# Spreading reciprocal roots over partitions: a store to DRAM and a broadcast read in place of eight products

## The chip, the cores and the metric

The kernel runs on one core of a Trainium2 chip. The metric is the device time of one execution in microseconds. PE is the engine of matrix products, DVE, ACT and POOL are the engines that work element by element, SP issues most of the DMAs. Each engine works through its own instructions in order, and waits where an instruction needs what another engine or a DMA has not finished. Profile lines name kernel lines as L381, and tiles by the program's names.

## What is computed

One layer of an encoder: RMS norm, one projection to q, k, v and a gate, two-dimensional neighbourhood attention, an output projection with the residual, and a last RMS norm. x has 2048 rows of 1024 numbers, all in float32.

```python
def rmsnorm(x, g):
    y = xf * lax.rsqrt(jnp.mean(xf * xf, axis=-1, keepdims=True) + RMS_EPS)
    return y * g

h = rmsnorm(x, norm_0)
q, k, v, gate = split(h @ w_in_0, 4)            # 1024 x 4096
o = neighbourhood_attention(q, k, v, rpb_0)     # 32 x 64 grid, windows of 8 x 16, 16 heads of 64
x = x + (o * silu(gate)) @ w_out_0
return rmsnorm(x, norm_f)
```

## The kernel before

**Products.** Each float32 factor is split into a rounded high part and a rest (ACT rounds, DVE subtracts, L445 and L446), and a product is made of three: high by high, high by rest, rest by high. Blocks of 128 by 512 are combined in the manner of Strassen, with seven products of blocks in place of eight (`seven_products`). One such product is twelve instructions on PE (L361). A unit is one pair of heads of q, k or gate: seven products in the order 1, 6, 2, 7, 5, 4, 3, in three PSUM banks that several of them share. Between them the results are read out: `keep` by ACT (L369), `add` by DVE (L374), `out_` by DVE (L379) with a product on POOL behind it (L381), `evac` by DVE (L296). A gate tile then goes through ACT (L307) and DVE (L308) and is stored by SP (L309); q and k are stored by SP (L314).

**Stages.** Stage one works on columns 0 and 1, the first 1024 rows of x transposed: first the values (`products_v`, L706), then twelve units, k of four pairs, and then q and gate in turn. Stage two works on the other 1024 rows: values first (`values_of`, L487, in four pairs of row tiles), then twelve units. Attention, the output projection and the last norm follow.

**Where the norm enters.** In stage one the products are made of x itself, times the gains, and the rows' reciprocal roots are multiplied in when the results leave PSUM: the tile rb[c] (c is 0 or 1) holds the 512 roots of column block c, the same on all 128 partitions. DVE reads it in `evac`, POOL in `out_`. Stage two multiplies rb[2] and rb[3] into the blocks of x before they are split (`normed`, L441).

**How rb is made.** The sums of squares are taken with rows on partitions (`square`), so the roots come out in rt with rows on partitions (`stats`: a few small instructions on DVE and POOL). To spread them, `diagonal(c)` multiplies the identity by four columns of rt on POOL and splits the result on ACT and DVE; `spread_rstd(c)` multiplies a tile of ones with both parts on PE and copies the result out of PSUM with ACT. For c of 0 and 1 it is written in the order in which k is stored (`lay("k", ...)`), and `reorder_rstd` rewrites it for q and gate when the four k units are done. The order matters because q, k and gate are stored in another order of rows than the one in which the products make them: `of` reads with a step of eight words, and `lay` writes runs:

```python
def of(kind, t):
    return t.rearrange("p (r c s) -> p r s c", c=8, s=8) if kind == "k" else t.rearrange("p (n s) -> p s n", s=8)
```

**What sets the order.** The schedule is written by hand. In the values of stage one a small planner places jobs between products: `job(ready, due, ops, f)` gives the earliest step, the due step and a cost of 2.8 steps for each op; a step is one instruction on PE. From there on, `also(n, i)` is called behind product i of unit n (n is 0 for the last unit of the stage), and `begun` holds functions for the first calls. In stage two, functions are handed to `pair` and called behind every twelve products of the values. Stores are put off by a number of products (`store(key, lag, f)`, carried out by `due`), and go to SP's queue at that point, so SP's order is the order of these calls. `ahead(i)` loads weights and forms factors of later products. Tiles are taken from pools that turn round: rb has three places, the first two of which are used by rows for the sums of squares and the third by a sum of the values.

Of the kernel before, what the change touches and what calls it, by code (L numbers as in the profile page):

```python
# [10 lines left out]
F32 = mybir.dt.float32  # L11
F32R = mybir.dt.float32r
BF16 = mybir.dt.bfloat16
I32 = mybir.dt.int32
AF = mybir.ActivationFunctionType
OP = mybir.AluOpType
# [44 lines left out]
def build(ctx, tc, x, xr, xt, wg, tab, w_out, n0, nf, out):  # L61
    nc = tc.nc
    ctx.enter_context(tc.manual_schedule())
    dram = ctx.enter_context(tc.tile_pool(name="dram", bufs=1, space=DRAM))
# [2 lines left out]
    sgd = [dram.tile([128, S], F32, name=f"sgd{p}") for p in range(NP)]  # L67
    vd = [dram.tile([4, S, 128], F32, name=f"vd{u}") for u in range(2)]
    ogd = [dram.tile([128, 4, NP, 128], F32, name=f"ogd{T}") for T in range(4)]
    wod = {f: dram.tile([128, 4, 2, 512], F32, name=f"wod{f}") for f in ("T1", "T2", "T3", "T4")}  # L70

    def pool(name, bufs):
# [3 lines left out]
    one = ctx.enter_context(tc.tile_pool(name="one", bufs=1))  # L76
# [27 lines left out]
    ev = pool("ev", 8)  # L104
    rbp = pool("rbp", 3)
# [3 lines left out]
    def bank(n, name):  # L109
        return banks.tile([128, n], F32, name=name, tag="bank")  # L110
# [5 lines left out]
        nc.tensor.matmul(zp, z[:, :128], z, start=True, stop=True)  # L116
    ident = one.tile([128, 128], F32, name="ident")
    make_identity(nc, ident)
    ones = one.tile([128, 128], F32, name="ones")
    nc.vector.memset(ones, 1.0)  # L120
    onesr = one.tile([128, 128], F32R, name="onesr")
    rt = one.tile([128, 16], F32, name="rt")
    rth = one.tile([128, 8], F32, name="rth")
    g0 = one.tile([128, NK], F32, name="g0")
# [15 lines left out]
    rb = {}  # L140
# [46 lines left out]
        if cs[0] < 2:  # L187
            nc.gpsimd.tensor_scalar(rth[:, 4 * cs[0]:4 * cs[0] + n], y, 0.5, 1.0, op0=OP.mult, op1=OP.mult)

    dgs = {}  # L190

    def diagonal(c):
        dg = ev([128, 512], F32, "dg")
        for i in range(4):
            nc.gpsimd.tensor_scalar(dg[:, i * 128:(i + 1) * 128], ident, rt[:, 4 * c + i:4 * c + i + 1], 1.0,
                                    op0=OP.mult, op1=OP.mult)
        dgs[c] = h, l = ev([128, 512], F32R, "dgh"), ev([128, 512], F32R, "dgl")
        nc.scalar.activation(h, dg, AF.Copy)
        nc.vector.tensor_tensor(l, dg, h.bitcast(F32), OP.subtract)

    def spread_rstd(c):
        p = bank(512, "prb")
        h, l = dgs.pop(c)
        nc.tensor.matmul(p, onesr, h, start=True, stop=False)
        nc.tensor.matmul(p, onesr, l, start=False, stop=True)
        rb[c] = rbp([128, 512], F32, "rb")
        if c < 2:
            nc.scalar.activation(lay("k", rb[c]), of("k", p), AF.Copy)
        else:
            nc.scalar.activation(rb[c], p, AF.Copy)  # L210

    def reorder_rstd(c):
        t = rbp([128, 512], F32, "rb")
        nc.scalar.activation(t.rearrange("p (s r c) -> p s r c", r=8, c=8),
                             rb[c].rearrange("p (r s c) -> p s r c", s=8, c=8), AF.Copy)
        rb[c] = t


    units_two = [(k, j) for j in range(4) for k in "kqg"]
    attending = [False]  # L220
# [42 lines left out]
    def of(kind, t):  # L263
        return t.rearrange("p (r c s) -> p r s c", c=8, s=8) if kind == "k" else t.rearrange("p (n s) -> p s n", s=8)

    def lay(kind, t):
        return t.rearrange("p (r s c) -> p r s c", s=8, c=8) if kind == "k" else t.rearrange("p (s n) -> p s n", s=8)
# [25 lines left out]

    def evac(kind, hp, c, p, then):
        tmp = ev([128, 512], F32, "tmp")
        nc.vector.tensor_tensor(lay(kind, tmp), of(kind, p), lay(kind, rb[c]), OP.mult)  # L296
        then.append(lambda: give(kind, hp, c, tmp))

    def give(kind, hp, c, t, bank_=False):
# [29 lines left out]
    def seven_products(us, c0, X1, also, lead=lambda i: 6, homes={}):  # L329
# [46 lines left out]
        def out_(n, a, c, P, u, then):  # L376
            kind, j = us[n]
            tmp = ev([128, 512], F32, "tmp")
            nc.vector.tensor_tensor(lay(kind, tmp), of(kind, B[n, P]), lay(kind, u), OP.add)  # L379
            if c0 == 0:  # L380
                nc.gpsimd.tensor_tensor(tmp, tmp, rb[c], OP.mult)  # L381
            then.append(lambda: give(kind, 2 * j + a, c, tmp))

        def ahead(i, more=0):
# [140 lines left out]
    def stage_one():  # L525
# [39 lines left out]
        begun = []  # L565

        def also(n, i):
            m = n + len(us) - 1
            if begun:
                begun.pop(0)()  # L570
            if (m, i) == (4, 0):
                reorder_rstd(0)
                reorder_rstd(1)
            if m < 8 and i == 2:
                more_rows[m] = xp([128, 512], F32, "row"), xp([128, 512], F32, "row")
                for j in range(2):
                    nc.sync.dma_start(more_rows[m][j], xr[(8 + m) * 128:(9 + m) * 128, 512 * j:512 * j + 512])
            if m < 8 and i == 6:
                for j, t in enumerate(more_rows.pop(m)):
                    square(8 + m, j, t)  # L580
                if m in (3, 7):
                    stats(2 + m // 4)
            if (n, i) == (-3, 1):
                diagonal(2)
            if (n, i) == (-3, 6):
                spread_rstd(2)
            if (n, i) == (-3, 5):
                spot2 = mkp([128, 3, 512], F32, "spot")
                L2["x11"] = [spot2[:, k] for k in range(3)] + [lp([128, 512], F32, "land")]
                for k in range(4):  # L590
                    load_x(2, "x11", k, L2["x11"][k])
            if (n, i) == (-2, 2):
                L2["x21"] = [xp([128, 512], F32, "land") for _ in range(4)]
                for k in range(4):
                    load_x(2, "x21", k, L2["x21"][k])
            if (n, i) in norms:
                f, k = norms[n, i]
                normed(f, 2, k, L2[f][k])
            if (n, i) == (-3, 4):
                diagonal(3)  # L600
            if n == 0:
                if i == 0:
                    for a, b in ((0, 0), (1, 0), (0, 1)):
                        load_v0(0, a, b)
                    X2["B11"] = [(xs([128, 512], F32R, "h"), xs([128, 512], F32R, "l")) for _ in range(4)]
                    for k in (0, 1):
                        split_to(*X2["B11"][k], L2["x11"][k], None)
                elif i == 1:
                    for a, b in ((1, 1), (0, 2), (1, 2)):
                        load_v0(0, a, b)  # L610
                    for k in (2, 3):
                        split_to(*X2["B11"][k], L2["x11"][k], None)
                    split_v(0, 0, 0)
                    split_v(0, 1, 0)
                elif i == 2:
                    X2["B21"] = [(xs([128, 512], F32R, "h"), xs([128, 512], F32R, "l")) for _ in range(4)]
                    split_v(0, 0, 1)
                elif i == 3:
                    split_v(0, 1, 1)
                    L2["x12"] = [vh([128, 512], F32, "land") for _ in range(4)]  # L620
                    for k in range(4):
                        load_x(2, "x12", k, L2["x12"][k])
                    for a in range(2):
                        load_v0(0, a, 3)
                elif i in (4, 5):
                    for k in (0, 1) if i == 4 else (2, 3):
                        split_to(*X2["B21"][k], L2["x21"][k], None)
                    if i == 5:
                        split_v(0, 0, 2)
                        split_v(0, 1, 2)  # L630
# [6 lines left out]
        parts_ = slice(0, 256), slice(256, 512)  # L637
        load_v0(0, 0, 0, cols=parts_[0], by=nc.scalar)
        load_x(0, "x11", 0, land["x11"][0], parts_[0])
        nc.scalar.activation(onesr, ones, AF.Copy)  # L640
        load_v0(0, 1, 0, cols=parts_[0])
        load_x(0, "x11", 0, land["x11"][0], parts_[1])
        load_v0(0, 0, 0, cols=parts_[1])
# [85 lines left out]
        def add_v(to, P, t, x, made=None):  # L729
            U[to, t] = made or U[x, t]  # L730
            nc.vector.tensor_tensor(U[to, t], B[bank_of[P], t], U[x, t], OP.add)
# [38 lines left out]
        def job(ready, due_, ops, f, *a):  # L770
            jobs.append((ready, due_, len(jobs), ops, f, a))
# [11 lines left out]
        for P, f, x, src, ready in ((5, "T1", t1, "x12", 46), (6, "T2", less, "x22", 84), (7, "T3", less, "x11", 130),  # L783
                                    (4, "T4", less, "x21", 130)):
            start = {5: 96, 6: 144, 7: 192, 4: 240}[P] - 12
# [29 lines left out]
            at(113 + 9 * i, square_rows, h)  # L815
        job(255, 255, .3, stats, 0, 1)
        at(250, ahead, -9)
        job(314, 303, 0.7, diagonal, 0)
        job(323, 312, 0.7, diagonal, 1)
        job(280, 284, 0, ahead, -8)  # L820
        job(282, 304, 1, ahead, -7)
        job(286, 308, 1, ahead, -6)
# [27 lines left out]
        for k in range(2):  # L850
            if k == 0:
                WV_["A11", 0] = wp([128, 2, 512], F32R, "wh"), wp([128, 2, 512], F32R, "wl")
                for h in range(2):
                    for a in ((1, 0) if h == 0 else ()):
                        t = raw_v("A11", a, 0).rearrange("p (k c) -> p k c", c=256)
                        s = slice(a * 256, a * 256 + 256)
# [11 lines left out]
            for a in range(2):  # L868
                t = raw_v("A11", a, 0).rearrange("p (k c) -> p k c", c=256)
                s = slice(a * 256, a * 256 + 256)  # L870
# [10 lines left out]
        while plan:  # L881
            plan.pop(0)[1]()
        VR.clear()
        begun.extend([lambda: [spread_rstd(0)] + [add_v(2, 3, t, 2) for t in (0, 1)],
                      lambda: [spread_rstd(1)] + [add_v(2, 3, t, 2) for t in (2, 3)]]
                     + [lambda ts=ts: [scaled(0, 4 + t, U, (2, t)) for t in ts] for ts in ((0, 1), (2, 3))])
        run()

# [875 lines left out]
```

## Time and profile before

| | |
|---|---|
| median of three runs | 1004.39 us (1003.68 to 1004.54) |
| the profiled execution | 1003.49 us, of which the span of the profile is 1001.7 us |
| busy: PE, DVE, ACT, POOL | 991.6, 727.5, 523.1, 197.7 us |
| granted clock of PE | 0.999 |
| stage one, values | to 83 us |
| stage one, units | 83 to 314 us |
| stage two, values and units | 314 to 588 us |

All figures below come from one profiled execution. The busy time of PE is a sum of pipelined instructions, and their rows are longer than the distance between two starts. In the rows of groups stand the line, the engine, the operation, the output and inputs, shape and count, then the busy time and the mean of one in ns, and then the idle time ahead of them with what ended it. In timelines the columns are the start and the length in us, the line and the operation; in brackets stands the idle time of the engine ahead of it, and what ended that. SPq stands for the DMAs that SP issues.

### The profile page before, as it was taken

To read this page: it belongs to the slowest core of one execution; us is meant where nothing else is said; L and a number is where in the kernel's file an instruction comes from. 1 tells how busy PE (TensorE), PEld (TensorE's weight loads), DVE (VectorE), ACT (ScalarE), POOL (GpSimd) and SP (SyncE) were. 2 spreads that over 40 slices of the span, in tenths; PEclk is the share of its full clock that TensorE was granted. 3 is DMA by queue.
4 is the path that set the end of the run, shared out by engine and by line. 5 is a ranking of instruction groups with operands and counts; after the bars stand their busy time and mean duration, and the time that the engine had idled before them with its cause. 6 is when DMAs were issued, how large, how long until landed. Compare 5 with 4: busy or idle time off the path is not lost.

```text
span 1001.7 us, 21635 instructions
## 1 busy us (share of the span) xinstructions
PE 991.6 (99%) x8080; PEld 802.0 (80%) x8080; DVE 727.5 (73%) x1557; ACT 523.1 (52%) x1316; POOL 197.7 (20%) x340
## 2 busy tenths in 40 slices
PE   9999999999999999999999999999999999999997
PEld 6888888888888888888888877777777777788885
DVE  6997666767798895776676565576767777666786
ACT  6767233333334452432433256777878777673253
POOL 0012323324321300000000012323333333320010
PEclk9999999999999999999999999999999999999999
DMA  9439445352736245655745588899988999989922
GB/s 315 135 96 271 139 138 146 118 157 92 202 91 205 76 142 151 220 183 170 236 162 160 167 250 285 298 329 348 299 269 282 316 309 294 318 282 354 355 94 84
DMA packets 124928, 213.82 MB, mean 213 GB/s; under 512 B 11352, under 2 KB 45528, under 8 KB 124824
## 3 DMA queue, kind: packets, MB, share of 16 engines
q1 hardware_dynamic: 123752, 209.96, 65.1%
q0 software_dynamic: 640, 2.10, 0.5%
q8 instruction: 63, 1.03, 0.4%
q14 instruction: 41, 0.34, 0.1%
q10 hardware_dynamic: 432, 0.40, 0.1%
HBM read 153.69 MB, written 58.72 MB: 212 GB/s over the span
## 4 chain that ended last, share of the span: by engine, by line
PE 90%; DVE 6%; issue 1%; ACT 1%; POOL 1%; DMA 0%; SPq 0%; DVEq 0%; ACTq 0%
PE pp L361 43%; PE o L1184 8%; PE pt L1463 7%; PE pv L706 7%; PE s L1120 6%; PE ph L1165 5%; PE pv L1019 5%; PE po L1379 3%; PE po L1383 3%; PE po L1381 3%; DVE l L446 1%; DVE land L441 1%; ACT h L445 1%; DVE land L963 1%; DMA raw<-in_wg_dram 0%
## 5 line engine op out<-in xcount | busy, mean ns | idle before, releaser
L361 PE MATMUL pp<-h,f 128*128 128x512 f32 x768 | 247.0, 389 | 0.8 <-DVE u L374 0.8
L361 PEld LDWEIGHTS pp<-h,f 128*128 128x128 f32 x768 | 144.2, 188 | 31.2 <-DVE u L374 1.2
L361 PE MATMUL pp<-four,f 128*128 128x512 f32 x648 | 156.8, 389 | 0.3 <-DVE u L374 0.3
L361 PE MATMUL pp<-l,f 128*128 128x512 f32 x384 | 149.5, 389 | 0.0
L361 PEld LDWEIGHTS pp<-four,f 128*128 128x128 f32 x648 | 121.5, 188 | 26.0 <-DVE u L374 0.9
L1148 POOL TENSOR_SCALAR x<-x,st 128x264 f32<-128x264 f32 (+1 forms) x192 | 96.7, 521 | 224.4 <-DVE st L1139 223.7
L1134 ACT ACTIVATE x<-x,st 128x264 f32<-128x264 f32 (+1 forms) x256 | 124.4, 487 | 21.2 <-DVE st L1129 21.2
L381 POOL TENSOR_TENSOR tmp<-tmp,rb 128x512 f32<-128x512 f32 x36 | 59.4, 1651 | 162.6 <-DVE tmp L379 128.2
L1129 DVE CUSTOM_DVE_ANT_0 x<-s,em 128x264 f32<-128x264 f32 (+1 forms) x256 | 89.4, 404 | 1.8 <-PE s L1120 1.8
L1168 DVE COPY pta<-ph 120x512 f32<-120x512 f32 (+5 forms) x96 | 56.0, 638 | 44.5 <-PE ph L1165 44.2
L1184 PEld LDWEIGHTS o<-pta,vt 120*64 120x64 f32 (+2 forms) x1024 | 68.5, 137 | 19.7 <-DVE st L1129 12.2
L361 PEld LDWEIGHTS pp<-l,f 128*128 128x128 f32 x384 | 72.1, 188 | 14.9
L1184 PE MATMUL o<-pta,vt 120*64 120x192 f32 (+5 forms) x1024 | 83.4, 316 | 0.0
L369 ACT ACTIVATE p<-pp 128x512 f32<-128x512 f32 x24 | 14.3, 597 | 120.4 <-PE pp L361 114.1
L1168 ACT ACTIVATE pta<-ph 120x512 f32<-120x512 f32 (+5 forms) x96 | 49.1, 558 | 43.9 <-PE ph L1165 43.9
L446 DVE TENSOR_TENSOR f<-raw,f 128x512 fp32r<-128x512 f32 x77 | 55.2, 719 | 23.2 <-ACT f L445 23.2
L1120 PE MATMUL s<-kt,qt 64*32 64x264 f32 (+1 forms) x2048 | 64.3, 374 | 0.0
L445 ACT ACTIVATE f<-raw 128x512 fp32r<-128x512 f32 x77 | 47.6, 624 | 30.3 <-PE pp L361 16.6
L379 DVE TENSOR_TENSOR tmp<-pp,u 128x512 f32<-128x512 f32 x48 | 33.1, 690 | 39.0 <-PE pp L361 34.4
L1165 PEld LDWEIGHTS ph<-ident,x 64*120 64x120 f32 (+2 forms) x1536 | 46.2, 128 | 11.3 <-issue 10.2
L361 PE MATMUL pp<-sixths,f 128*128 128x512 f32 x216 | 52.9, 389 | 0.0
L1165 PE MATMUL ph<-ident,x 64*120 64x64 f32 (+2 forms) x1536 | 50.7, 219 | 0.0
(246 smaller groups left out, 1855.6 us busy)
## 6 DMA issues: line engine op xcount, KB each, us to landing
raw<-in_wg_dram SPq DMA_DIRECT2D x120, 256.0 KB, 4.6
em<-in_tab_dram SPq DMA_DIRECT2D x16, 912.0 KB, 7.8
em<-in_tab_dram SPq DMA_DIRECT2D x16, 528.0 KB, 7.3
row<-in_xr_dram SPq DMA_DIRECT2D x32, 256.0 KB, 3.4
sgd<-sg SPq DMA_DIRECT2D x32, 256.0 KB, 2.8
qt<-qd SPq DMA_DIRECT2D x32, 256.0 KB, 5.5
sgt<-sgd SPq DMA_DIRECT2D x32, 256.0 KB, 8.8
ogd<-og SPq DMA_DIRECT2D x32, 256.0 KB, 4.0
```

The source lines that it names most:

```text
L361: nc.tensor.matmul(B[n, P], t[:, int(m == 2), c], x[k][int(m == 1)], start=P in (1, 6, 5) and k == 0 and m == 0, stop=k == 3 and m == 2, s ...
L381: nc.gpsimd.tensor_tensor(tmp, tmp, rb[c], OP.mult)
L446: nc.vector.tensor_tensor(l, t, h.bitcast(F32), OP.subtract)
L706: nc.tensor.matmul(B[bank_of[P], t], a[:, t * 128:t * 128 + 128], b, start=P == bank_of[P] and k == 0 and m == 0, stop=k == 3 and m == 2, ...
L1120: nc.tensor.matmul(pst[s][h * 32:h * 32 + 32], qt[e, q:q + 32], keys.rearrange("p r (s c) -> p s r c", c=8), start=True, stop=True)
L1129: nc.vector.tensor_tensor_reduce(X[i, C][s], ps, em, -1.0, 1e38, OP.add, OP.min, st[:, o:o + 1])
L1134: nc.scalar.activation(X[i, C][s], X[i, C][s], AF.Exp, bias=st[:, o:o + 1], scale=-1.0, accum_out=st[:, 4 + o:5 + o])
L1148: nc.gpsimd.tensor_scalar(X[i, C][s], X[i, C][s], st[:, o:o + 1], 1.0, op0=OP.mult, op1=OP.mult)
L1165: nc.tensor.transpose(to_, XF[2 * m + C // 2, C][s][q, j * k:j * k + k], ident[q, q])
L1168: (nc.vector.tensor_copy if h else lambda o, i_: nc.scalar.activation(o, i_, AF.Copy))(to[:k, :, 2 - j, h, c], at[h][:k, :, c])
L1184: nc.tensor.matmul(o[s * 64:s * 64 + 64, g0 * 64:g1 * 64 + 64].rearrange("d (g q) -> d g q", q=64), vt[:k, strip, s * 64:s * 64 + 64], t[: ...
L1463: nc.tensor.matmul(B[n, P], t[:, int(m == 2), c], WO[uses[P][1], k][int(m == 1)], start=P in (1, 6, 5) and k == 0 and m == 0, stop=k == 3 ...
```

## The change

The roots are stored to DRAM in the order of rows and read back by all 128 partitions at once. `diagonal`, the eight products with ones, the copies out of PSUM, `reorder_rstd` and the tiles ones and onesr are gone. `store_rstd` is issued on POOL, the read on SP. rb now always lies in the order of rows, so `evac` and `out_` read it with `of`, by a step of eight words. The reads of rb[0] and rb[1] move from behind the first product of the units into the planned part; those of rb[2] and rb[3] stay at their places in the order of calls.

```diff
+    rd = [dram.tile([512], F32, name=f"rd{c}") for c in range(4)]
...
-    ones = one.tile([128, 128], F32, name="ones")
-    nc.vector.memset(ones, 1.0)
-    onesr = one.tile([128, 128], F32R, name="onesr")
...
-    def diagonal(c):
...
+    def store_rstd(*cs):
+        for c in cs:
+            nc.gpsimd.dma_start(rd[c].rearrange("(t p) -> p t", p=128), rt[:, 4 * c:4 * c + 4])
 
     def spread_rstd(c):
-        p = bank(512, "prb")
-        h, l = dgs.pop(c)
-        nc.tensor.matmul(p, onesr, h, start=True, stop=False)
-        nc.tensor.matmul(p, onesr, l, start=False, stop=True)
         rb[c] = rbp([128, 512], F32, "rb")
-        if c < 2:
-            nc.scalar.activation(lay("k", rb[c]), of("k", p), AF.Copy)
-        else:
-            nc.scalar.activation(rb[c], p, AF.Copy)
-
-    def reorder_rstd(c):
...
+        nc.sync.dma_start(rb[c], bass.AP(tensor=rd[c].tensor, offset=rd[c].offset, ap=[[0, 128], [1, 512]]))
...
     def evac(kind, hp, c, p, then):
-        nc.vector.tensor_tensor(lay(kind, tmp), of(kind, p), lay(kind, rb[c]), OP.mult)
+        nc.vector.tensor_tensor(lay(kind, tmp), of(kind, p), of(kind, rb[c]), OP.mult)
...
             if c0 == 0:
-                nc.gpsimd.tensor_tensor(tmp, tmp, rb[c], OP.mult)
+                nc.gpsimd.tensor_tensor(lay(kind, tmp), lay(kind, tmp), of(kind, rb[c]), OP.mult)
...
-            if (m, i) == (4, 0):
-                reorder_rstd(0)
-                reorder_rstd(1)
...
             if (n, i) == (-3, 1):
-                diagonal(2)
+                store_rstd(2)
             if (n, i) == (-3, 6):
                 spread_rstd(2)
...
             if (n, i) == (-3, 4):
-                diagonal(3)
+                store_rstd(3)
...
-        nc.scalar.activation(onesr, ones, AF.Copy)
...
-        job(314, 303, 0.7, diagonal, 0)
-        job(323, 312, 0.7, diagonal, 1)
+        job(285, 280, 0, store_rstd, 0, 1)
+        job(296, 280, 0, spread_rstd, 0)
+        job(297, 280, 0, spread_rstd, 1)
...
-        begun.extend([lambda: [spread_rstd(0)] + [add_v(2, 3, t, 2) for t in (0, 1)],
-                      lambda: [spread_rstd(1)] + [add_v(2, 3, t, 2) for t in (2, 3)]]
+        begun.extend([lambda: [add_v(2, 3, t, 2) for t in (0, 1)],
+                      lambda: [add_v(2, 3, t, 2) for t in (2, 3)]]
```

`spread_rstd(3)` is not in the diff's lines: it is called in stage two, behind the first twelve products of the values, together with the split of a weight (`both(w(0, 3), lambda: spread_rstd(3))`).

More of the change, by code (lines that the diff above doesn't have):

```diff
@@ L188, in stats @@
             nc.gpsimd.tensor_scalar(rth[:, 4 * cs[0]:4 * cs[0] + n], y, 0.5, 1.0, op0=OP.mult, op1=OP.mult)
-    dgs = {}
-    def diagonal(c):
[L193 to L199, printed above, removed]
+    def store_rstd(*cs):
+        for c in cs:
+            nc.gpsimd.dma_start(rd[c].rearrange("(t p) -> p t", p=128), rt[:, 4 * c:4 * c + 4])
     def spread_rstd(c):
-        p = bank(512, "prb")
-        h, l = dgs.pop(c)
-        nc.tensor.matmul(p, onesr, h, start=True, stop=False)
-        nc.tensor.matmul(p, onesr, l, start=False, stop=True)
         rb[c] = rbp([128, 512], F32, "rb")
-        if c < 2:
-            nc.scalar.activation(lay("k", rb[c]), of("k", p), AF.Copy)
-        else:
-            nc.scalar.activation(rb[c], p, AF.Copy)
-    def reorder_rstd(c):
[L213 to L216, printed above, removed]
+        nc.sync.dma_start(rb[c], bass.AP(tensor=rd[c].tensor, offset=rd[c].offset, ap=[[0, 128], [1, 512]]))
     units_two = [(k, j) for j in range(4) for k in "kqg"]
```

## The prediction

> **What bounds the kernel now.** I read the engine totals, then PE's waits, then the chain that ended last:
>
> ```profile
> PE 991.6 (99%) x8080; PEld 802.0 (80%) x8080; DVE 727.5 (73%) x1557; ACT 523.1 (52%) x1316; POOL 197.7 (20%) x340
> ```
> ```profile
> PE pp L361 <- DVE u L374: 1.1, 2, 0.8
> ```
> ```profile
> 89.68 141.50 PE pp L361 x624
> ```
>
> PE hardly ever waits: on the projection products it stopped twice, 1.1 us in all, both times for the DVE sum at L374. The third row is a stretch of the chain: 624 products in 141.50 us, one each 0.227 us. So a product taken out of PE's order is worth 0.227 us, as long as nothing else comes due. The two stops show where something does. The first, in the timelines of PE, POOL, ACT and DVE:
>
> ```profile
> 248.01 2.20 PE L361 MATMUL pp<-sixths,f 128*128 128x512 f32 x9
> 250.97 0.50 PE L361 MATMUL pp<-h,f 128*128 128x512 f32 x1 [0.77 <-DVE u L374]
> ```
> ```profile
> 245.71 0.37 POOL L195 TENSOR_SCALAR dg<-ident,rt 128x128 f32<-128x128 f32 x1
> ```
> ```profile
> 247.16 0.63 ACT L198 ACTIVATE dgh<-dg 128x512 fp32r<-128x512 f32 x1 [5.63 <-POOL dg L195]
> ```
> ```profile
> 247.82 0.69 DVE L199 TENSOR_TENSOR dgl<-dg,dgh 128x512 fp32r<-128x512 f32 x1 [3.54 <-ACT dgh L198]
> ```
>
> Here diagonal(2) makes the stop: its products with the identity stand on POOL behind the Newton steps of stats, ACT stands 5.63 us for them, DVE 3.54 us for ACT, and PE pays. The ninth product started at 248.01 + 8 x 0.227 = 249.82, the next was due at 250.05 and started at 250.97: 0.92 us. The second stop ends a chain that runs through the place where rb[3] is first used (L441):
>
> ```profile
> 317.39 1.63 POOL tmp L381
> ...
> 319.04 0.64 ACT sg L307
> ...
> 321.60 0.68 DVE land L441
> ...
> 366.23 0.61 DVE u L374
> ```
> ```profile
> 366.88 0.97 PE L361 MATMUL pp<-four,f 128*128 128x512 f32 x3 [0.31 <-DVE u L374]
> ```
>
> From 317.39 to 366.88 the chain is on POOL, ACT and DVE alone, with PE busy beside it and nothing to spare: PE stopped at its end. What delays DVE in this stretch delays the kernel by as much, and what frees PE there frees nothing.
>
> **The change, part by part.** *Eight products go.* 8 x 0.227 = 1.81 us of PE. The last pair, that of spread_rstd(3), stands beside the DVE chain:
>
> ```profile
> L204 PE MATMUL prb<-dgh,onesr x4: 404/404/404, 85.8 to 316.9; 128*128 128x512 f32 x4
> ```
>
> At 316.9 us its 0.45 us is not gained: -1.36 us.
>
> *The diagonals go*, with 16 POOL, 4 ACT and 4 DVE instructions and six ACT copies of rb. Without diagonal(2), DVE has 3.54 us of idle time and 0.69 us of dgl back ahead of a stop of 0.92 us: -0.92 us. The rest lies beside PE work that does not wait: nothing. The two planned diagonal jobs held four steps of the plan (0.9 us), so later jobs move up by that, beside PE: nothing. ones and onesr go at the start, where ACT's next work waits for a DMA anyway: nothing.
>
> *Four stores from POOL*, each of 512 separate words. The nearest row, POOL's stores of the output:
>
> ```profile
> L1494 POOL DMA_DIRECT2D out_dram<-t x8: 539/542/732, 957.3 to 971.3; - x8
> ...
> DMA to landing us min/median/max: 2.0/2.3/2.5
> ```
>
> 128 rows take 0.54 us on POOL and 2.3 us to land; for four times as many pieces I bound it by 0.54 and 2.2 us on POOL, 2 and 4.5 us to land. [...] The first two stores hold SP, because the reads of rb[0] and rb[1] are now queued ahead of the load of A12 into acc, of the stores of values and of three weight loads. SP's timeline, then POOL's and ACT's:
>
> ```profile
> 61.98 0.94 SPq L339 DMA_DIRECT2D acc<-in_wg_dram  x2
> 74.30 0.39 SPq L715 DMA_DIRECT2D vd<-u  x1
> ```
> ```profile
> 70.77 0.54 POOL L188 TENSOR_SCALAR rth<-rt 128x8 f32<-128x8 f32 x1
> ```
> ```profile
> 83.23 0.61 ACT L445 ACTIVATE f<-acc 128x512 fp32r<-128x512 f32 x1
> ```
>
> POOL is free at 71.3; the first store lands at 73.3 to 75.8, SP then issues the read and the second acc load (at 62 us now), which has landed some 3 us later, at 77 to 80. It is used at 83.23 now and perhaps 2.5 us sooner afterwards. The stores behind slip by 2 to 5 us and have no reader near. I take nothing; if the cover is gone, the price is at most the 1 or 2 us by which A12 is late. Stores 2 and 3 stand on POOL where the diagonals stood, with 5 us or more before their reads are queued: nothing.
>
> *The read of rb[3] comes late.* It is queued after twelve products of stage two; on SP that is behind both last stores of the gate, and the second of them waits for DVE's L308. SP's timeline, DVE's, and the time to landing of the L438 loads of 256 KB between 296 and 345 us:
>
> ```profile
> 317.88 2.87 SPq L309 DMA_DIRECT2D sgd<-sg  x2
> 333.72 5.50 SPq L321 DMA_DIRECT2D vd<-v  x4
> ```
> ```profile
> 319.71 0.69 DVE L308 SCALAR_TENSOR_TENSOR sg<-sg,tmp 128x512 f32<-128x512 f32 x1 [1.85 <-ACT sg L307]
> 320.32 1.29 DVE L470 TENSOR_TENSOR wl<-raw,wh 128x512 fp32r<-128x512 f32 x2
> 321.52 0.75 DVE L441 SCALAR_TENSOR_TENSOR land<-land,g,rb 128x512 f32<-128x512 f32 x1
> ```
> ```profile
> DMA to landing us min/median/max: 3.0/5.2/5.3
> ```
>
> SP is done with the gate at 317.88 + 2.87 = 320.75. With the quickest landing rb[3] is there at 323.75, while DVE wants it at 321.52: 2.2 us, with all splits of B12 and B22 and the sums of stage two queued behind on DVE, and ACT waiting for DVE. I take the quickest, because SP issues nothing more until 333 us; the median would make it 4.4. The chain carries it to PE: +2.2 us.
>
> *POOL and DVE now read rb with a step of eight words.* The nearest rows: POOL's product with two inputs (page), POOL's with one, DVE with a stepped PSUM input, and DVE without:
>
> ```profile
> L381 POOL TENSOR_TENSOR tmp<-tmp,rb 128x512 f32<-128x512 f32 x36 | 59.4, 1651 | 162.6 <-DVE tmp L379 128.2
> ```
> ```profile
> 995.36 0.68 POOL L1499 TENSOR_SCALAR og<-og,st 128x512 f32<-128x512 f32 x1 [23.50 <-ACT st L1486]
> ```
> ```profile
> L379 DVE TENSOR_TENSOR tmp<-pp,u 128x512 f32<-128x512 f32 x48 | 33.1, 690 | 39.0 <-PE pp L361 34.4 <-POOL tmp L381 3.7 <-issue 0.9
> ...
> L350 DVE TENSOR_TENSOR s<-raw 128x512 f32<-128x512 f32 x24 | 16.4, 684 | 0.0
> ```
>
> A stepped read costs DVE nothing from PSUM (690 against 684 ns); from SBUF I bound it by 0 and by a doubling, 0.69 us, and take 0, since the twelve instructions at L296 do not stand in the chain. For POOL I call the extra x and bound it by 0 and by the price of a whole second input, 1.65 - 0.68 = 0.97 us; nearer to the DVE rows than to another input, I take x = 0.4. It is not hidden, since DVE instructions with two SBUF inputs stand until POOL's product ends:
>
> ```profile
> 309.73 1.66 POOL L381 TENSOR_TENSOR tmp<-tmp,rb 128x512 f32<-128x512 f32 x1 [10.91 <-DVE tmp L379]
> ```
> ```profile
> 309.57 2.38 DVE L446 TENSOR_TENSOR l<-land,h 128x512 fp32r<-128x512 f32 x2
> ```
> ```profile
> 278.55 1.77 DVE L449 SCALAR_TENSOR_TENSOR f<-raw,f 128x512 fp32r<-128x512 f32 x1
> 282.94 0.69 DVE L374 TENSOR_TENSOR u<-pp,p 128x512 f32<-128x512 f32 x1
> ```
> ```profile
> 284.28 3.56 PE L361 MATMUL pp<-four,f 128*128 128x512 f32 x15
> ```
>
> Two L446 take 2.38 us, where two L470 took 1.29, ending just after POOL's 311.39. At the head of the chain this happens twice, and the third time ACT and then DVE wait for POOL itself (317.39): 3x = 1.2 us, at the same place as rb[3] and added to it. The gate unit before holds DVE three times too (the last is shown); the L374 behind ends at 283.63, and PE needs its bank at 284.28: of 1.2 us, 0.65 is hidden and 0.55 is paid.
>
> Sum: -1.36 - 0.92 + 2.2 + 1.2 + 0.55 = +1.7 us. The profiled execution took 1003.49 us (span 1001.7), 0.9 below the median of the runs; on the median, 1004.4 + 1.7 = 1006.1 us. About 0.2%, 2.0 us, is what a measurement of this kernel tells from no change, so this is no change, near its upper edge.
>
> **The rivals.** *Slower: POOL pays heavily for the step.* Beyond x = 0.45 the sum, -0.08 + 3x + (3x - 0.65), passes 2 us. For it: POOL pays 0.97 us for a second input, DVE nothing like it. Against it: nothing but the DVE rows. [...]
>
> *The step costs POOL nothing.* Then -0.08: 1004.3 us, rb[3]'s wait against the products and the stop.
>
> *Faster: PE keeps the bound.* If rb[3] lands within 0.7 us of SP's issue, or the splits behind it catch up before PE needs them, and x is small, -1.81 - 0.92 remains: 1001.7 us. Against it: no load of the window landed in under 3.0 us, and the chain has no gap to catch up in.
>
> **How the numbers follow.** My forecast (x from 0.2 to 0.45) 0.40; POOL heavier 0.35; step free 0.15; PE keeps the bound 0.10. A wait for rb[3] near the median instead of the quickest moves a part of the forecast, 0.07, over the edge. Faster 0.10, same 0.33 + 0.15 = 0.48, slower 0.35 + 0.07 = 0.42. The likeliest one's own range is 1005.0 to 1007.5. The range: below, 1003 leaves out most of the faster rival; above, 1010 takes in x = 0.97, which gives -0.08 + 5.82 - 0.65 = +5.1 (1009.5).
>
> **What would show it.** Right: no wait of PE near 250 us; the first L441 after the gate's last L308 waits about 2 us for a DMA named rb; L381 near 2.05 us instead of 1.65; PE's one long stop, or two that share it, at the first products of stage two, 3 to 4 us together; a small one near 282. Wrong: L441 finding rb[3] landed; L381 unchanged or past 2.4 us; L296 well above the 0.69 us of DVE's other rows and in the chain; a PE stop before 100 us, behind A12 or the first rb; or a later first product, if the table load that came with onesr now follows a wait.

## The result, and the profile after

The changed kernel took 1018.17 us (median of four runs, 1017.77 to 1018.56), the kernel before, run beside it, 1004.03 us (1002.92 to 1004.54): a ratio of 1.0137, interval 1.0124 to 1.0149. It is slower by 14.1 us, where I forecast +1.7 and a range that ended at +5.6. The profiled execution took 1017.8 us, its span 1016.0, against 1001.7 before.

The waits of PE after the change, with the time in all, the count, and the longest:

```profile
PE pp L338 <- DVE u L351: 7.3, 2, 6.3
PE pp L338 <- DVE f L423: 4.7, 1, 4.7
PE pp L338 <- ACT p L346: 1.5, 1, 1.5
```

L338, L351 and L423 are L361, L374 and L446 of before. Before, PE stopped for 1.1 us in all on these products; now it stops for 13.5. To place the loss I set each product on PE against the same product of the kernel before (every matrix instruction except those with onesr) and took the difference of their start times. What it grows by in each stretch sums to what PE's last product is late:

| stretch, in times of before | measured, us | forecast, us |
|---|---|---|
| start to 84 us | +1.14 | 0 |
| 84 to 100 us, two pairs of products gone | +8.64 | -0.90 |
| 251 us, the stop of diagonal(2) | -1.06 | -0.92 |
| 257 us, the pair of c=2 | -0.53 | -0.45 |
| 284 us, the gate unit | +1.35 | +0.55 |
| 300 to 380 us, the pair of c=3 and the start of stage two | +5.45 | +3.40 |
| the rest | -0.73 | 0 |
| sum | +14.26 | +1.68 |

Most of the rest is one step of -0.87 us at 855 us, where PE pauses in the trace of before without a cause that the profile shows; nothing of the change is near it.

Of the 14 us, 8.6 arose in a stretch for which I forecast a gain. The table by windows shows it; the columns are the window, its length, the busy time of PE, PEld, DVE, ACT and POOL, the granted clock, the share of the DMA engines and GB/s. First the kernel before, then after:

```profile
85.00:110.00 25.00, 25.00 (x112) 20.57 (x111) 19.90 (x29) 12.99 (x26) 4.88 (x3) 1.00 0.71 209
```
```profile
85.00:110.00 25.00, 17.24 (x70) 13.46 (x68) 13.29 (x20) 12.28 (x23) 1.47 (x1) 0.86 1.04 289
94.00:101.00 7.00, 0.72 (x3) 0.42 (x2) 3.02 (x6) 1.69 (x3) 0.00 (x0) 0.69 1.05 279
101.00:104.00 3.00, 3.00 (x9) 2.33 (x9) 3.00 (x6) 1.86 (x4) 0.00 (x0) 0.59 0.84 231
```

In the same 25 us PE starts 70 products in place of 112, and the granted clock falls to 0.69 and 0.59 around the longest stop: between 101 and 104 us only nine products start in 3 us, where at 0.227 us each there would be thirteen. What the change holds up there is SP. Its waits from 55 to 110 us, its timeline, and the rows of the store:

```profile
SPq L194 <- DMA rd<-rt: 18.9, 2, 17.8
```
```profile
63.11 0.33 SPq L316 DMA_DIRECT2D acc<-in_wg_dram  x1
81.32 0.33 SPq L194 DMA_DIRECT2D rb<-rd  x1
81.75 0.37 SPq L316 DMA_DIRECT2D acc<-in_wg_dram  x1
83.67 0.33 SPq L194 DMA_DIRECT2D rb<-rd  x1
...
91.36 1.62 SPq L316 DMA_DIRECT2D raw<-in_wg_dram  x3
```
```profile
L190 POOL DMA_DIRECT2D rd<-rt x4: 768/799/957, 72.4 to 262.7; - x4
...
DMA to landing us min/median/max: 8.9/10.7/14.0
```

SP comes to the first read (L194) at 63.5 us and stands there for 17.8 us. POOL issues the store at 72.39, but its landing is seen only at 81.3. The second load of A12 goes out at 81.75 (62 us before), the three weight loads behind the stores of values at 91.36 (79.50 before). The readers stand for them, ACT and then DVE:

```profile
88.27 0.63 ACT L422 ACTIVATE f<-acc 128x512 fp32r<-128x512 f32 x1 [6.91 <-DMA acc<-in_wg_dram]
```
```profile
97.98 0.69 DVE L327 TENSOR_TENSOR s<-raw 128x512 f32<-128x512 f32 x1 [5.51 <-DMA raw<-in_wg_dram]
```

DVE's L351, for whose bank PE waits 6.3 us, stands behind the second row. The second loss is at stage two; SP, DVE, PE:

```profile
328.09 3.21 SPq L286 DMA_DIRECT2D sgd<-sg  x2
331.39 0.38 SPq L194 DMA_DIRECT2D rb<-rd  x1
```
```profile
335.77 0.75 DVE L418 SCALAR_TENSOR_TENSOR land<-land,g,rb 128x512 f32<-128x512 f32 x1 [3.62 <-DMA rb<-rd]
```
```profile
372.56 0.79 PE L338 MATMUL pp<-h,f 128*128 128x512 f32 x2 [4.67 <-DVE f L423]
...
373.58 1.05 PE L338 MATMUL pp<-h,f 128*128 128x512 f32 x2
374.43 0.63 PE L338 MATMUL pp<-l,f 128*128 128x512 f32 x1
```

This is the chain that the prediction described, with a wait of 3.62 us in place of 2.2, and something more: behind the stop two products take 0.85 us (373.58 to 374.43), 0.425 each in place of 0.227. The read of rb[2] made SP stand too, at 263 us, though nothing was priced there:

```profile
SPq L194 <- DMA rd<-rt: 5.9, 1, 5.9
```

Products were slow behind both long stops: behind the one of 6.3 us the granted clock was 0.59 from 101 to 104 us, behind the one of 4.7 us 0.51 from 373 to 376 us. Shorter stops differed: one of 2.2 us in the fourth experiment and those near 90 us in the first (2.1 and 1.5 us) left the granted clock of their windows at 1.00, one of 1.9 us in the ninth went with 0.93 from 85 to 110 us.

Rows for the steps of eight words (POOL's from the page, with the mean of one in ns; DVE's with the shortest, median and longest), and one each for the gate unit and the start:

```profile
L358 POOL TENSOR_TENSOR tmp<-tmp,rb 128x512 f32<-128x512 f32 x36 | 72.1, 2004 | 169.0 <-DVE tmp L356 160.6
```
```profile
L273 DVE TENSOR_TENSOR tmp<-pp,rb x12: 1110/1130/1157, 102.8 to 314.7; 128x512 f32<-128x512 f32 x12
```
```profile
293.68 3.69 PE L338 MATMUL pp<-four,f 128*128 128x512 f32 x15 [1.05 <-DVE u L351]
```
```profile
3.17 1.28 ACT L425 ACT_TABLE_LOAD   x1 [3.17 <-DMA land<-in_xt_dram]
```

### The profile page after: what moved, and what is told of

Read it like the earlier page. It is cut to its first block, busy times and chain, and to the rows that moved or that the text cites. A ratio compares the mean times of both kernels' runs of the same rounds, so it can differ in the third digit from the quotient of the medians.

```text
span 1016.0 us, 21614 instructions
## 1 busy us (share of the span) xinstructions
PE 992.9 (98%) x8072; PEld 801.8 (79%) x8072; DVE 738.7 (73%) x1552; ACT 516.9 (51%) x1305; POOL 206.6 (20%) x328
## 4 chain that ended last, share of the span: by engine, by line
PE 62%; DVE 5%; issue 1%; DMA 1%; ACT 1%; POOL 0%; SPq 0%; DVEq 0%; ACTq 0%
PE pp L338 23%; PE o L1158 8%; PE pt L1437 7%; PE s L1094 6%; PE ph L1139 5%; PE pv L993 5%; PE po L1353 3%; PE po L1357 3%; PE po L1355 3%; DVE land L418 1%; DVE l L423 1%; ACT h L422 1%; DVE land L937 0%; DMA rb<-rd 0%; DMA sgd<-sg 0%
## 5 line engine op out<-in xcount | busy, mean ns | idle before, releaser
L338 PE MATMUL pp<-h,f 128*128 128x512 f32 x768 | 248.0, 391 | 6.2 <-DVE f L423 4.7
L338 PEld LDWEIGHTS pp<-h,f 128*128 128x128 f32 x768 | 144.8, 189 | 37.1 <-DVE f L423 5.1
L338 PE MATMUL pp<-four,f 128*128 128x512 f32 x648 | 158.3, 392 | 7.3 <-DVE u L351 7.3
L338 PE MATMUL pp<-l,f 128*128 128x512 f32 x384 | 150.2, 391 | 0.0
L338 PEld LDWEIGHTS pp<-four,f 128*128 128x128 f32 x648 | 122.5, 190 | 33.8 <-ACT u L695 6.7
L358 POOL TENSOR_TENSOR tmp<-tmp,rb 128x512 f32<-128x512 f32 x36 | 72.1, 2004 | 169.0 <-DVE tmp L356 160.6
L338 PEld LDWEIGHTS pp<-l,f 128*128 128x128 f32 x384 | 72.4, 188 | 15.0
L423 DVE TENSOR_TENSOR f<-raw,f 128x512 fp32r<-128x512 f32 x77 | 55.4, 722 | 23.3 <-ACT f L422 23.3
L338 PE MATMUL pp<-sixths,f 128*128 128x512 f32 x216 | 52.9, 389 | 0.0
```

The costliest lines, as they stand in the source:

```text
L338: nc.tensor.matmul(B[n, P], t[:, int(m == 2), c], x[k][int(m == 1)], start=P in (1, 6, 5) and k == 0 and m == 0, stop=k == 3 and m == 2, s ...
L358: nc.gpsimd.tensor_tensor(lay(kind, tmp), lay(kind, tmp), of(kind, rb[c]), OP.mult)
L423: nc.vector.tensor_tensor(l, t, h.bitcast(F32), OP.subtract)
```

## The experiments

The theory was that three things of the change cost the time: reads that hold SP behind a slow store (theory 1 in the first expectations), the late read of rb[3], and the stepped reads of rb. Rivals were the moved table load and the slow issue of the store on POOL. All differences below are against the changed kernel unless another one is named.

**1. The reads of rb[0] and rb[1] go back to where the spreads were,** behind the first two products of the units.

```diff
-        job(296, 280, 0, spread_rstd, 0)
-        job(297, 280, 0, spread_rstd, 1)
...
-        begun.extend([lambda: [add_v(2, 3, t, 2) for t in (0, 1)],
-                      lambda: [add_v(2, 3, t, 2) for t in (2, 3)]]
+        begun.extend([lambda: [spread_rstd(0)] + [add_v(2, 3, t, 2) for t in (0, 1)],
+                      lambda: [spread_rstd(1)] + [add_v(2, 3, t, 2) for t in (2, 3)]]
```

> The changed kernel with the reads of rb[0] and rb[1] put back behind the first two products of the units, so that SP does not stand for the store ahead of A12, the value stores and the weight loads. Theory 1 (SP held for the landing of the store makes the stop at 89 to 101 us): the two stops there go, some 8.7 us with PE's slow restart, 1018.2 falls to about 1009.5 us, and the second acc load is issued near 63 us. Theory 2 (the stop comes from the diagonals missing in the order of ACT and DVE, or from tiles that turn round differently): the stop stays, 1018 us.

Measured: 1012.2 us, ratio to before 1.0085 (1.0068 to 1.0102), 6.0 us less than the changed kernel. SP no longer waits for the store, and the stretch from 84 to 100 us loses 3.1 us in place of 8.6. But it should have gained 0.9. SP's timeline shows what is left:

```profile
77.99 6.28 SPq L688 DMA_DIRECT2D vd<-u  x2
```

The same two issues, of stores that have nothing to do with the roots, took 1.27 us before. SP is slow inside an instruction and not in a wait. So a second cost hides behind the first.

**2. The store issued by ACT's queue** (`nc.scalar.dma_start` in place of `nc.gpsimd.dma_start`).

> The changed kernel with the four stores issued from ACT's queue in place of POOL's, 512 single words as before. If the single words make the landing slow (theory P), it stays near 9 us and so does the stop near 90 us: 1017 to 1019 us. If POOL's way of issuing makes it slow (theory Q), it lands in 2 to 3 us, SP goes on near 76 us, and the time falls by 6 to 9 us.

Measured in a single run: 1020.32 us. The issues are shorter, the landing is not:

```profile
L190 ACTq DMA_DIRECT2D rd<-rt x4: 366/378/525, 71.9 to 259.4; - x4
...
DMA to landing us min/median/max: 10.3/10.8/13.4
```

POOL's issuing is not what is slow. The page also shows the pieces: on the queue that carries ACT's DMAs there are 2112 packets more than before, 528 for each store of 512 words. The row of that queue, before and in this run (queue, packets, MB, share):

```profile
q10 hardware_dynamic: 432, 0.40, 0.1%
```
```profile
q10 hardware_dynamic: 2544, 0.41, 0.2%
```

**3. The store in runs of 16 bytes.** Each partition's four roots are stored side by side, the same bytes in 128 pieces. What it leaves out is to put them back in order: the read is as before, so rows get the roots of other rows, with the same work.

```diff
-            nc.gpsimd.dma_start(rd[c].rearrange("(t p) -> p t", p=128), rt[:, 4 * c:4 * c + 4])
+            nc.gpsimd.dma_start(rd[c].rearrange("(p t) -> p t", p=128), rt[:, 4 * c:4 * c + 4])
```

> The changed kernel with the stores laid out so that each partition writes one run of 16 bytes: 128 pieces in place of 512. The roots then stand in another order in DRAM, which leaves the amount of work as it is. Theory P: the landing falls with the number of pieces, to 2 to 4.5 us, and the stop near 90 us shrinks by 5 us or more. Theory Q: the landing stays near 9 us, and the time near 1018 us.

Measured in a single run: 1010.79 us. Landing, and the first read on SP:

```profile
L190 POOL DMA_DIRECT2D rd<-rt x4: 551/582/738, 71.7 to 254.3; - x4
...
DMA to landing us min/median/max: 2.2/3.9/5.7
```
```profile
73.88 0.33 SPq L194 DMA_DIRECT2D rb<-rd  x1
```

2.2 us to land in place of 8.9. With SP still waiting, the stretch from 84 to 100 us loses 0.9 us in place of 8.6. The form of the store is the root of that loss; the place of the reads decides how much of it is felt.

**4. The step alone:** the kernel before, spread by products, with rb in the order of rows and read by `of` in `evac` and `out_`; `reorder_rstd` is gone.

> The kernel before, with one part of the change: rb in the order of rows (still spread by products), and read with a step of eight words by DVE and POOL, the reorder gone. If the step is paid at the head of stage two and in the gate unit at 284 us, as in the changed kernel's trace (POOL 2.0 instead of 1.65 us, DVE 1.13 instead of 0.69): three times 0.35 at the first place and about 1.2 at the second, 1004.0 + 2.2 = 1006.2 us. If it is hidden: 1004.0 us.

Measured: 1008.54 us, ratio 1.0044 (1.0029 to 1.0059), 4.2 us over before, twice what was expected. Its trace, of the fastest of its runs, ends 3.46 us late. Of these, 0.99 fall at stage two (the forecast's 3x was 1.2) and 0.56 at the gate unit (forecast 0.55), but 1.48 at 250 us, where POOL's longer products push diagonal(2) back:

```profile
PE pp L358 <- DVE u L371: 2.2, 1, 2.2
```

That part can't arise in the changed kernel, which has no diagonal. Another 1.27 us came behind 880 us and -0.87 at 855; neither is explained.

**5. The read of rb[3] queued early,** at (-1,0), into a buffer that is free there.

```diff
-        rb[c] = rbp([128, 512], F32, "rb")
+        rb[c] = (more if c == 3 else rbp)([128, 512], F32, "rb")
...
+            if (n, i) == (-1, 0):
+                spread_rstd(3)
...
-        pair(0, (8, 9), both(w(0, 3), lambda: spread_rstd(3)), block("B12", x12, 0, 1), block("B12", x12, 2, 3),
+        pair(0, (8, 9), w(0, 3), block("B12", x12, 0, 1), block("B12", x12, 2, 3),
```

> The changed kernel with one edit: the read of rb[3] is queued at the start of the last unit of stage one, into a tile that is free there, some 27 us ahead of its use. If the wait for it is what made the stop at the first product of stage two's units (4.8 us, and PE's slow restart behind it, 1.5 us), the 3.6 us of that wait go, the stop shrinks to 1.2 us or less, the restart goes, and the time falls from 1018.2 to about 1013 us. If the DVE chain is long for other reasons (POOL's step, ACT), the wait moves to another row and the time stays above 1016 us.

Measured: 1013.68 us, ratio to before 1.0095 (1.008 to 1.011), 4.5 us less than the changed kernel. The waits of PE:

```profile
PE pp L338 <- DVE u L351: 7.2, 3, 6.2
PE pp L338 <- ACT p L346: 1.9, 1, 1.9
PE pp L338 <- DVE f L423: 1.0, 1, 1.0
```

The stop behind L423 shrinks from 4.7 to 1.0 us, within the 1.2 that was expected. More goes than the 3.62 us of DVE's wait, because the slow products behind the stop go with it: the window from 355 to 380 us has a granted clock of 1.00, where the changed kernel had 0.93.

```profile
355.00:380.00 25.00, 23.36 (x102) 18.71 (x101) 24.64 (x36) 15.32 (x30) 5.05 (x3) 1.00 0.32 95
```

**6. ones, onesr and the table load put back** at the start.

> The changed kernel with ones and onesr put back, which nothing reads: ACT's table load then stands ahead of the first wait again. If the load behind the wait made the first product late, it starts at 4.5 us again in place of 5.3, and the time falls by 0.8 to 1.1 us, to 1017.2. If the start is covered by loads that come later anyway, 1018.2 us.

Measured: 1019.43 us, ratio to before 1.0153 (1.013 to 1.0176): no gain. The first product starts at 4.69 us in place of 5.33, and at 84 us PE is 1.05 us ahead of the changed kernel; it loses that again at the two stops (10.5 us in place of 8.6 from 84 to 100 us, 6.7 in place of 5.5 at stage two). In all six traces without ones the first product is 0.8 to 1.15 us later than before, in the other eight at most 0.2. But that is not what is left at 84 us: without ones PE is there from 0.2 us ahead of before (experiment 5) to 1.4 late (experiment 8), with them from level to 0.4 late, and once 3.1 late (experiment 11, whose start is that of before). So the moved load shows at the first product, and a price in the time is not shown.

**7. One term alone:** the kernel before, with diagonal(2) moved from (-3,1) to (-3,4) and diagonal(3) from there to (-2,0).

> The kernel before with one thing changed: the diagonal of c=2 is built three products later (where c=3's was) and that of c=3 four products later still; the spreads stay. It isolates one term of the prediction, the 0.92 us stop of TensorE at 250 us that its trace puts down to the diagonal. If POOL's diagonal is what delays the product there, the stop goes and the time falls by 0.9 us, to about 1003.2 (ratio 0.999); if the stop has another cause it stays, and the time is 1004.0.

Measured: 1003.0 us beside 1003.93, ratio 0.9989 (0.998 to 0.9998). The stop at 250 us is gone; from 200 to 400 us PE waits only for

```profile
PE pp L361 <- DVE u L374: 0.3, 1, 0.3
```

The stop was the diagonal's, and to be had without the change. Of 1.06 us won at 251 us, this wait gives 0.3 back at 257; the interval of the time allows a gain of 0.2 to 2.0 us.

**8. The step removed for q and gate:** ACT rewrites rb[0] and rb[1] at (4,0), as `reorder_rstd` did.

> The changed kernel with rb[0] and rb[1] rewritten by ACT into the order of q and gate when the four k units are done, so that POOL and DVE read runs again in the eight units behind. If the step is the price, L358 falls from 2.0 to 1.65 us there, the stop at 293 us (1.2 us) goes, the stop of stage two shrinks by 1.05 us: 1016 us. If not, 1018 us.

Measured in a single run: 1017.02 us, 1.2 us less. In the trace stage two loses 4.4 us in place of 5.45, as expected, but the gate unit still loses 0.67 in place of 1.35: the step is not all that it pays. POOL's products fall back to

```profile
L358 POOL TENSOR_TENSOR tmp<-tmp,rb x36: 1592/1670/2092, 109.5 to 327.2; 128x512 f32<-128x512 f32 x36
```

**9. The edits of 1, 5, 6 and 8 together,** still with single words.

> The changed kernel with four edits together: reads of rb[0] and rb[1] behind the first products, rb[3] read early, ones and onesr back, and the rewriting for q and gate. The single words of the stores stay. If the four costs are those of the single runs and nothing else stands against the eight products (1.81) and the stop of the diagonal (0.92), only what the stores still hold up near 90 us is left, about 4 us: 1004.0 - 2.7 + 4 = 1005.3 us. If the costs overlap in one chain, so that one of them alone is paid where two stood, it stays near 1008 us.

Measured: 1007.2 us, ratio 1.0032 (1.0016 to 1.0047): 11.0 us gained, still slower than before, and 1.9 us above the 1005.3 that was expected. PE's longest stops that are left are 1.9 us at 91 and 2.4 us at 275 us; the gate unit loses 1.13 us, without any step there. Ahead of the second, SP stands for a store of q:

```profile
SPq L418 <- DMA qd<-tmp: 8.1, 1, 8.1
```

That is behind the store of the roots of c=3, issued at 255.7 us and landed 17.4 us later. Again a transfer that shares nothing with the roots lands late.

**10. The single words by themselves:** the kernel before, plus the stores of c=0 and c=1, which nothing reads.

```diff
+        job(285, 280, 0, store_rstd, 0, 1)
         job(314, 303, 0.7, diagonal, 0)
```

> The kernel before, with nothing taken away and two transfers added: the stores of the roots of c=0 and c=1 in single words, from POOL, at the same place as in the changed kernel. Nothing reads them and nothing waits for them. If single words hold back the other transfers (the kernel with late reads lost 4.0 us near 90 us though nothing of its queue stood behind a wait), the stops near 90 us appear here too, some 2 to 4 us, and the time is 1006 to 1008.5. If only who waits for them is hurt, it stays at 1004.0, and the 4.0 us there came from the reads.

Measured: 1007.37 us, ratio 1.0036 (1.0022 to 1.005). The rows of the stores of values between 70 and 95 us, the kernel before and then this one, with their times to landing:

```profile
L715 SPq DMA_DIRECT2D vd<-u x12: 359/377/610, 74.3 to 94.4; - x12
...
DMA to landing us min/median/max: 2.2/2.4/4.5
```
```profile
L720 SPq DMA_DIRECT2D vd<-u x8: 360/382/5333, 74.6 to 91.9; - x8
...
DMA to landing us min/median/max: 2.6/7.5/9.8
```

The median landing goes from 2.4 to 7.5 us, and one issue took 5.33 us, with 4 KB of roots in single words on the way. From 77 to 81 us the DMA engines are as good as busy throughout and move almost nothing; the windows of before, of this kernel, and of experiment 13, which has these two stores in runs of 16 bytes (the last two columns are the share of the DMA engines, which can pass 1, and GB/s):

```profile
77.00:81.00 4.00, 4.00 (x19) 3.33 (x18) 3.26 (x6) 3.13 (x6) 3.26 (x6) 1.00 1.16 348
```
```profile
77.00:81.00 4.00, 4.00 (x19) 3.34 (x18) 2.33 (x4) 2.35 (x4) 0.00 (x0) 1.00 0.93 14
```
```profile
77.00:81.00 4.00, 4.00 (x19) 3.31 (x18) 3.27 (x6) 4.00 (x9) 0.00 (x0) 1.00 1.15 345
```

POOL's diagonal, which reuses a tile that such a store holds, pays for it, and ACT, DVE and PE behind it:

```profile
84.50 3.77 POOL L196 TENSOR_SCALAR dg<-ident,rt 128x128 f32<-128x128 f32 x8 [11.26 <-DMA vd<-u]
```

In the kernel before it began at 76.71 us. The stretch from 84 to 100 us loses 3.8 us. This shows the contention without a wait of the change's own.

**11. c=2 and c=3 alone by DRAM, in the kernel before.** The rows of x for their sums of squares are loaded as row 4p+t, so the runs of 16 bytes are in the right order; rb[3] is read at (-1,0).

```diff
+        nc.gpsimd.dma_start(rd[c].rearrange("(p t) -> p t", t=4), rt[:, 4 * c:4 * c + 4])
...
-                    nc.sync.dma_start(more_rows[m][j], xr[(8 + m) * 128:(9 + m) * 128, 512 * j:512 * j + 512])
+                    nc.sync.dma_start(more_rows[m][j], xr[1024 + m // 4 * 512:1536 + m // 4 * 512, 512 * j:512 * j + 512].rearrange("(p t) d -> t p d", t=4)[m % 4])
```

> The kernel before, with c=2 and c=3 alone spread by DRAM. The rows that their roots are computed from are loaded as row 4p+t, so that each partition's four roots are neighbours and the store is 128 runs of 16 bytes; the read of rb[3] is queued at (-1,0), ahead of its first use by some 20 us, into a buffer that is free there. The roots of c=0 and c=1 are spread by products as before, so the start, the natural order and the stretch at 80 to 100 us are untouched. Theory (the loss is in the single words, the early blocking reads and the late rb[3]; what the change set out to save is real): four products of 0.23 us and the 0.92 us stop go, 1002.2 to 1002.7 (ratio 0.998). Rival (a store and a read cost something in any form, where weights are streaming): 1004 or more.

Measured: 1002.69 us, ratio 0.9989 (0.9981 to 0.9998). That is where the theory put it, and below the rival's 1004. The gain is hardly more than that of experiment 7 (1003.0), so it doesn't show by itself what the products are worth.

**12. All repairs and runs of 16 bytes:** the edits of 9, and the rows and the store of 11 for every c.

> The changed kernel with all repairs: reads of rb[0] and rb[1] behind the first two products, rb[3] read at (-1,0) into a free buffer, the table load at its old place, natural order for the gate and query units, and the stores as runs of 16 bytes (the rows of c=2 and c=3 loaded to fit; those of c=0 and c=1 are not, so their roots come out in another order, with the same work). Beside the same with single words (1007.2) it shows what the words still cost there: its stops of 2.3 us at 91 and 2.8 us at 275 should go, and with the eight products and the stop at 250 saved the time should be 1002 to 1003.5. If the words are not the cause, 1006 to 1007.

Measured: 1000.75 us, ratio 0.9973 (0.9961 to 0.9984), 6.4 us less than with single words and 1.25 below the lower end that was expected. The roots of c=0 and c=1 are not yet in the order in which they are read.

**13. The same, with the roots of c=0 and c=1 put in order by ACT.** Both reads go behind the first product, and ACT writes them in the order of the tokens behind the second.

```diff
+    def in_order(c):
+        t = rbp([128, 512], F32, "rb")
+        nc.scalar.activation(t.rearrange("p (t q) -> p t q", t=4), rb[c].rearrange("p (q t) -> p t q", t=4), AF.Copy)
+        rb[c] = t
...
+        begun.extend([lambda: [spread_rstd(0), spread_rstd(1)] + [add_v(2, 3, t, 2) for t in (0, 1)],
+                      lambda: [in_order(0), in_order(1)] + [add_v(2, 3, t, 2) for t in (2, 3)]]
```

> The changed kernel with all repairs, now with every root in its right place: for c=0 and c=1 the store is in runs of 16 bytes, which leaves the roots in the order 4p+t; both are read behind the first product into short-lived tiles, and ACT writes each in the order of the tokens (two 128x512 rewrites of about 1.2 us) behind the second. Theory (the loss came from the single words, the reads that held SP, and the late rb[3]; nothing else): the rewrites are hidden, ACT being busy for 11.7 of the 25 us at 85 to 110 us, and the time is that of the version without them, 1000.3 to 1001.5 (ratio 0.997). Rival (ACT, which takes its work in order, waits for the reads to land and sends the weight splits behind them late): a stop of 1 to 3 us near 92 us, 1002 to 1004.

Measured: 1000.72 us (1000.02 to 1000.86), ratio 0.9963 (0.9949 to 0.9977), faster than both kernels. The rewrites, PE's waits on the projection products, and two windows:

```profile
L201 ACT ACTIVATE rb<-rb x2: 1114/1126/1138, 91.3 to 92.3; 128x512 f32<-128x512 f32 x2
```
```profile
PE pp L346 <- DVE u L359: 0.7, 1, 0.7
```
```profile
85.00:110.00 25.00, 25.00 (x112) 20.72 (x111) 22.21 (x29) 13.29 (x24) 5.71 (x3) 1.00 0.79 241
240.00:270.00 30.00, 30.00 (x134) 24.86 (x133) 21.29 (x33) 7.88 (x14) 11.08 (x18) 1.00 0.60 174
```

PE is busy throughout in both. At 380 us its products are 2.26 us ahead of before, with 0.31 lost at the start; the prediction's two savings were 1.36 + 0.92 = 2.28. Another 0.87 us of its lead is the step at 855 us that the first table has under the rest, and not the change's.

## Why the prediction was wrong

**The step that failed** is the part on the four stores: "I bound it by 0.54 and 2.2 us on POOL, 2 and 4.5 us to land", and "I take nothing; if the cover is gone, the price is at most the 1 or 2 us by which A12 is late". The time on POOL held (0.77 to 0.96 us), the landing did not: 8.9 to 14.0 us. The bounds came from 128 long pieces, scaled by the count of pieces; the row that they rest on had no single words in it, and an end of the range that no row carries should not have been closed at 4.5. Experiment 2 counts the pieces: 528 packets for a store of 512 words. Three further mistakes stand in the same part. A12 was rounded at 88.27 us, 5.0 us late and not 1 or 2. And I listed three weight loads among what SP was held back from, and then priced only the values' stores ("have no reader near"): the loads went out 11.9 us late, and PE's longest stop is theirs. And I put stores 2 and 3 at nothing, with 5 us of cover; the read of rb[2] stood 5.9 us for a landing of 11.5. Last, the transfers did not only stand behind a wait: the words made others slow, which experiment 10 shows by itself and the prediction did not consider. From 84 to 100 us the words alone cost 3.8 us (experiment 10), SP's wait alone, with runs, 2.0 (experiment 3, 0.9 against the -1.1 of experiments 12 and 13), and both together 9.7 (8.6 against the same -1.1).

**What no term held:** the slow products behind the two long stops. At 0.425 in place of 0.227 us, each product of the stretch that followed cost 0.2 us more; at stage two (granted clock 0.51 from 373 to 376 us) that took the delay from 13.85 to 15.57 us, 1.7 of the 5.5 us there.

**The late rb[3]** was right in place and cause, and small: 3.62 us against 2.2. The quickest landing was the wrong choice; from the issue at 331.39 to the first use at 335.77 it took 4.4 us, beside 3.0 to 5.3 us of the quoted loads. With the clock that makes 4.5 us (experiment 5).

**The step for POOL** was right: x = 2004 - 1651 ns = 0.35 us by the means of the two pages, against 0.4. It is 21%, so the rival that POOL pays heavily was not what made the kernel slower. **The step for DVE** was not: 692 to 1130 ns, 0.44 us where I took 0; the stepped PSUM read (690 against 684 ns) was no measure for the one from SBUF. It is not why the gate unit paid 1.35 us and not 0.55: in experiments 3 and 4 both engines step and no single words are on the way, and the unit pays 0.57 and 0.56, as forecast. With single words it pays 0.67 and 1.13 without the step (8 and 9), and 0.61 to 1.54 with it (the changed kernel, 1, 2, 5 and 6). So what comes on top comes with the words alone, and differs from run to run.

**The savings** were right: eight products and the stop at 250 us, -2.28 us by the forecast and -2.26 at 380 us in experiment 13; experiment 7 has the stop alone, -0.9 us. **The start** was put at nothing; the first product is 0.8 us late in the changed kernel, the lag is 1.14 us at 84 us, and experiment 6 got no time back for it.

What stays open: the steps at 855 us and behind 880 us (experiments 4 and 10), and why single words slow other transfers. The profile counts only 128 packets more on POOL's queue for the four stores, in words and in runs alike; for ACT's queue it counts the pieces (experiment 2). That the DMA engines move almost nothing for some microseconds while words are on the way is shown, what keeps them is not.

## What to carry to other kernels

Look at the smallest piece that a transfer writes, not at its bytes: two stores of 2 KB in single words cost 3.4 us with nobody reading them, paid by whoever else had a transfer on the way. Before moving a wait into a queue that issues loads, list every load behind it to the first reader and price the latest, not the next. And when a change loses, take its parts one by one: what it set out to save was there, and wider stores, later and earlier reads, and rewrites by ACT made a loss of 14 us into a gain of 3.4, of which the traces tie some 2.3 to the change.

## What the hardware showed that I had not expected

Stores of 128x4 words to separate places landed in 8.9 to 14.0 us from POOL (17.4 in experiment 9) and 10.3 to 13.4 from ACT's queue, in runs of four words in 2.2 to 5.7 (experiment 3). While the words were on the way, other stores landed in 7.5 us in place of 2.4, and the DMA engines, counted as 93% busy, moved 14 GB/s in place of 348 (experiment 10). A step of eight words in the SBUF input made a DVE product of 128x512 take 1130 ns in place of 692, with the same step in its PSUM input both times; the step in PSUM alone cost nothing (690 against 684 ns). POOL paid 0.35 us. Behind stops of PE of 4.7 and 6.3 us, products ran at 0.425 us each in place of 0.227.
